# Two weight pieces of an output projection in other buffers, and one shared buffer for the first turned probabilities of each head

## The chip, the cores and the metric

The kernel runs on one core of one Trainium2 chip. The metric is the device time of one execution in microseconds (us).

## The reference

One layer of a streaming encoder, for 1024 tokens of width 1024 and 256 memory tokens, in float32:

```python
# 1. token mixing: u, q, k, v, f = rms_norm(x) @ w_in, then
y_s = s5_mixer(u)                          # 32 groups x 16 channels, gated
y_f = forgetting_attention(q, k, v, f)     # 8 heads x 64, blocks of 128 queries, causal
y = concatenate([rms_norm(y_s), rms_norm(y_f)]) @ w_out
x = x + rms_norm(y, post_g)
# 2. cross-attention, 4 heads of 256, over 256 memory tokens
x = x + rms_norm(memory_cross_attention(rms_norm(x), mem_n, wq, wkv, wo))
# 3. x = x + rms_norm(swiglu(rms_norm(x), w_gate, w_up, w_down))
```

## The kernel before

**Products.** Every float32 product is made from a hi and a lo part: `split` writes hi on ScalarE (L113) and lo, the source less hi, on VectorE (L115; L117 where a gain is multiplied in), and three matmuls (L122 to L124) sum hi·hi, hi·lo and lo·hi. A 128 x 1024 weight piece is loaded by SyncE into a staging buffer (512 KB), split into a buffer of 8 KB per partition that holds both parts, and then multiplied.

**Buffers.** The pool `slab` has 16 buffers of 8 KB, `raw` (staging) 2, `whl` (split pieces) 3. The pool `t4` has buffers of 4 KB by tag: a 2, b 2, c 3, d 1, e 1, and smaller ones, t2 3 and yt 2. A new tile of a tag takes the oldest buffer, and whatever writes it first (mostly a load) waits until the old tile's last reader is done. PSUM has four banks `g` and, once attention is over, four banks `x`.

**Order.** The kernel is written once, and a scheduler with a timeline of its own decides in what order the instructions stand on each engine. Within an engine, and in SyncE's row of loads, the order is then fixed: what waits holds up everything behind it.

**Attention** (`fox`) runs 8 heads of 8 query tiles. `scores` makes probabilities in a tile `c`; `turn` transposes them on TensorE (L771) and splits the result into hi and lo for a pair of query tiles; `values` multiplies them with v (L782, L783). The squares of the result (ScalarE, L802) are summed by GpSimd (L803) into `d`, summed over channels by TensorE (L237), and give `r_f`, the scale of this branch for each token. Beside attention other work is stepped through as filler, among it cross-attention's `build_a`, which multiplies the query weights (`in_wqT`, loaded by `load_w`, L158) with the memory's keys.

**Output projection** (`wo` and the loop below it). The state-space half was done before and lies in HBM as `t1_d` (`t_d` in the profile). For the attention half, `w_out_f` comes in 4 pieces, staged in `raw` and split into `slab` (L1029). Then for each of 8 token tiles j: `xt` in a buffer c is loaded from x (L1038), `t` from `t1_d` (L1041); 2 x 12 products go into two banks `x`; VectorE adds them, scaled by `r_f`, onto `t` (L1048); ScalarE squares (L1050), GpSimd multiplies by a gain row (L1052); the squares are summed (L1054), and VectorE's last step (L1056) adds `t`, scaled, to `xt`, which GpSimd's queue stores (L1057). So `t` of tile j holds its buffer from its load to L1056. Its tag is "aab"[j % 3]: tiles 0, 1, 3, 4, 6, 7 take the two buffers a, tiles 2 and 5 take b.

**Behind it** stands cross-attention's value side: `wo` of cross-attention comes in pieces through `raw` and `e` (`raw<-in_wo`, `e<-in_wo`), is split into `whl`, and is multiplied into banks `g` and `x` (`g<-whl,b`, `x<-whl,b` at L122 to L124).

Of the kernel before, what the change touches and what calls it, by code (L numbers as in the profile page):

```python
# [17 lines left out]
P = 128  # L18
S = 1024
D = 1024  # L20
# [32 lines left out]
def layer(ctx: ExitStack, tc: tile.TileContext, a, out):  # L53
# [15 lines left out]
    def slab(shape, dt=F32R):  # L69
        return slabp.tile(shape, dt, name="slab", tag="slab")  # L70
# [4 lines left out]
    def raw(shape):  # L75
        return rawp.tile(shape, F32, name="raw", tag="raw")

    def g_ps(shape):
        return psg.tile(shape, F32, name="g", tag="g")
# [4 lines left out]
    def sm(n, name):  # L84
        return small.tile([P, n], F32, name=name, tag=name)
# [26 lines left out]
    def split(hi, lo, src, mul=None, lo_eng=None):  # L112
        first = act.activation(out=hi, in_=src, func=AF.Copy, scale=1.0 if mul is None else mul)  # L113
        if mul is None:
            (lo_eng or dve).tensor_tensor(out=lo, in0=src, in1=hi.bitcast(F32), op=ALU.subtract)  # L115
        else:
            dve.scalar_tensor_tensor(out=lo, in0=src, scalar=mul, in1=hi.bitcast(F32),  # L117
                                     op0=ALU.mult, op1=ALU.subtract)
        return first

    def mm3(ps, lh, ll, rh, rl, first, last):
        pe.matmul(ps, lh, rh, start=first, stop=False)  # L122
        pe.matmul(ps, lh, rl, start=False, stop=False)  # L123
        pe.matmul(ps, ll, rh, start=False, stop=last)  # L124

    def rsqrt_mean(r, ss, n, eps=EPS, ahead=None):

        w = r.shape[1]
        y, t, v = sm(w, "rsy"), sm(w, "rst"), sm(w, "rsv")
        if ahead is None:  # L130
            bias, half = epsc[:, 0:1] if eps == EPS else epsc[:, 1:2], -0.5 * eps
        else:
            e = sm(2, "rse")
            bias, half = e[:, 0:1], e[:, 1:2]
            dve.tensor_scalar(out=bias, in0=ahead, scalar1=1.0 / n, scalar2=eps, op0=ALU.mult, op1=ALU.add)
            dve.tensor_scalar(out=half, in0=bias, scalar1=-0.5, scalar2=None, op0=ALU.mult)
        act.activation(out=y, in_=ss, func=AF.Ln, scale=1.0 / n, bias=bias)
        last = act.activation(out=y, in_=y, func=AF.Exp, scale=-0.5)
        dve.tensor_scalar(out=v, in0=ss, scalar1=-0.5 / n, scalar2=half, op0=ALU.mult, op1=ALU.add)
        if w == 1:  # L140
            dve.scalar_tensor_tensor(out=t, in0=y, scalar=v, in1=y, op0=ALU.mult, op1=ALU.mult)
        else:
            dve.tensor_tensor(out=t, in0=y, in1=y, op=ALU.mult)
            dve.tensor_tensor(out=t, in0=t, in1=v, op=ALU.mult)
        done = dve.scalar_tensor_tensor(out=r, in0=t, scalar=1.5, in1=y, op0=ALU.add, op1=ALU.mult)
        return last, done
# [48 lines left out]
    def tt(tag, shape=None, dt=F32):  # L195
        return t4.tile(shape or [P, S], dt, name=tag, tag=tag, bufs=BUFS[tag])
# [508 lines left out]
    def fox(yf):  # L705
        heads, units, pts = {}, {}, {}
# [54 lines left out]
        def turn(h, t):  # L761
            tt = t % 2
            if tt == 0:
                pts[h, t // 2] = slab([P, 8, 256]), slab([P, 8, 256])
            pth, ptl = pts[h, t // 2]
            sc = units.pop((h, t))
            for k0 in range(0, t + 1, 4):
                n = min(4, t + 1 - k0)
                tp = g_ps([P, 4, P])
                for k in range(n):  # L770
                    pe.transpose(tp[:, k], sc[:, (k0 + k) * P:(k0 + k + 1) * P], ident)  # L771
                split(pth[:, k0:k0 + n, tt * P:(tt + 1) * P], ptl[:, k0:k0 + n, tt * P:(tt + 1) * P], tp[:, :n])
# [45 lines left out]
        for n in range(-lag, len(seq) + 1):  # L818
            if n + lag < len(seq):
                h, t = seq[n + lag]  # L820
                scores(h, t)
                if t == 1 and h + 1 < NH:
                    nxt = prepare(h + 1)
                if t % 2 and h + 1 < NH:
                    step(nxt)
                if t == 5 and h % 2 and h + 1 < NH:
                    load_v(h // 2 + 1)
            if 0 <= n < len(seq):
                h, t = seq[n]
                turn(h, t)  # L830
            yield
            if 0 < n:
                h, t = seq[n - 1]
                if t % 2:
                    values(h, t // 2)
                    if len(later) > 1 or h >= HA and later:
                        token_sums(*later.pop(0))
# [30 lines left out]
    def step(g, n=1):  # L868
        for _ in range(n):
            if next(g, "end") == "end":  # L870
                return
# [151 lines left out]
    def x_ps(shape):  # L1023
        return psx.tile(shape, F32, name="x", tag="x")

    wo = []
    for i in range(4):
        w = raw([P, D])
        sp.dma_start(out=w, in_=a["w_out_f"][i])  # L1029
        hl = slab([P, 2, D])  # L1030
        split(hl[:, 0], hl[:, 1], w)
        wo.append(hl)
    g_mp = gain_row(0, "d")
    a1 = build_a(1)
    for j in range(NT):
        ts = slice(j * P, (j + 1) * P)
        xt = tt("c")
        sp.dma_start(out=xt, in_=a["x"][ts, :])  # L1038
        t = tt("aab"[j % 3])
        for i in range(2):  # L1040
            sp.dma_start(out=t[64 * i:64 * i + 64], in_=t1_d.rearrange("j (k s) d -> s k j d", s=16)[2 * j + i])  # L1041
        ss4, ss, r = sm(4, "ss4"), sm(1, "ss"), sm(1, "r")
        for h in range(2):
            hs = slice(h * 512, h * 512 + 512)
            ps = x_ps([P, 512])
            for k in range(4):
                mm3(ps, yf[k][:, 0, ts], yf[k][:, 1, ts], wo[k][:, 0, hs], wo[k][:, 1, hs], k == 0, k == 3)
            dve.scalar_tensor_tensor(out=t[:, hs], in0=ps, scalar=r_f[:, j:j + 1], in1=t[:, hs], op0=ALU.mult, op1=ALU.add)  # L1048
            for q in range(2 * h, 2 * h + 2):
                act.activation(out=tt("yt", [P, 256]), in_=t[:, q * 256:q * 256 + 256], func=AF.Square,  # L1050
                               accum_out=ss4[:, q:q + 1])
            pool.tensor_tensor(out=t[:, hs], in0=t[:, hs], in1=g_mp[:, hs], op=ALU.mult)  # L1052
            step(a1)
        dve.tensor_reduce(out=ss, in_=ss4, op=ALU.add, axis=mybir.AxisListType.X)  # L1054
        rsqrt_mean(r, ss, D)
        dve.scalar_tensor_tensor(out=xt, in0=t, scalar=r, in1=xt, op0=ALU.mult, op1=ALU.add)  # L1056
        stC.dma_start(out=x1_d[j], in_=xt)  # L1057
# [13 lines left out]
    xT, xr, pts, x1_read = {}, {}, {}, []  # L1071
# [235 lines left out]
    def ev():  # L1307
        return evp.tile([P, 512], F32, name="ev", tag="ev")
# [111 lines left out]
    for n in range(2):  # L1420
        w = ev()
# [185 lines left out]
```

## Time and profile before

| | before |
|---|---|
| median of 3 runs (lowest to highest) | 1432.37 us (1430.96 to 1433.04) |
| the profiled execution's own time | 1430.57 us |
| its span | 1428.8 us |
| mean granted TensorE clock | 0.992 |
| TensorE busy | 1390.7 us, 97% |
| VectorE, ScalarE, GpSimd busy | 70%, 50%, 29% |

The profile shows one execution; its times are counted from the start of its span. In a row, a name before `<-` is written and names behind it are read, with the numbers of buffers left out. A bracket behind a row is the time that the engine stood idle before it and the instruction that released it. The granted clock of TensorE is 1.00 at full speed.

### The profile page before, as it was taken

To read this page: it belongs to the slowest core of one execution; us is meant where nothing else is said; L and a number is where in the kernel's file an instruction comes from. 1 tells how busy PE (TensorE), PEld (TensorE's weight loads), DVE (VectorE), ACT (ScalarE), POOL (GpSimd) and SP (SyncE) were. 2 spreads that over 40 slices of the span, in tenths; PEclk is the share of its full clock that TensorE was granted. 3 is DMA by queue.
4 is the path that set the end of the run, shared out by engine and by line. 5 is a ranking of instruction groups with operands and counts; after the bars stand their busy time and mean duration, and the time that the engine had idled before them with its cause. 6 is when DMAs were issued, how large, how long until landed. Compare 5 with 4: busy or idle time off the path is not lost.

```text
span 1428.8 us, 20846 instructions
## 1 busy us (share of the span) xinstructions
PE 1390.7 (97%) x7422; PEld 1187.5 (83%) x7422; DVE 1003.7 (70%) x1818; ACT 708.0 (50%) x1421; POOL 410.9 (29%) x432
## 2 busy tenths in 40 slices
PE   7999999999999898999999999999999999999997
PEld 6889898889989886788888788888888888888886
DVE  7839947877888876645557677887766676565565
ACT  6373347777888754543434533333333334444341
POOL 0001000022243134001111367676666661000021
PEclk9999999999999999999999999999999999999999
DMA  6325654165654658323637455454444446965444
GB/s 204 98 80 148 183 192 132 33 204 178 193 153 120 172 164 276 134 74 109 193 112 236 149 190 173 168 181 154 164 156 162 162 155 227 334 219 192 177 162 162
DMA packets 112824, 238.43 MB, mean 167 GB/s; under 512 B 11848, under 2 KB 48712, under 8 KB 112592
## 3 DMA queue, kind: packets, MB, share of 16 engines
q1 hardware_dynamic: 96576, 182.01, 39.8%
q0 software_dynamic: 16144, 55.09, 10.6%
q8 instruction: 58, 0.95, 0.3%
q14 instruction: 46, 0.38, 0.1%
HBM read 168.90 MB, written 76.81 MB: 172 GB/s over the span
## 4 chain that ended last, share of the span: by engine, by line
PE 58%; DVE 1%; DMA 1%; ACT 0%; issue 0%; DVEq 0%; SPq 0%; ACTq 0%
PE x L1277 17%; PE g L1277 13%; PE x L1535 7%; PE g L1535 7%; PE x L123 2%; PE x L124 2%; PE x L122 2%; PE g L122 2%; PE g L124 2%; PE g L123 2%; PE g L1065 1%; DMA a<-t_d 1%; PE g L1173 1%; DVE slab L115 0%; DVE whl L115 0%; DVE c L1056 0%
## 5 line engine op out<-in xcount | busy, mean ns | idle before, releaser
L1277 PE MATMUL x<-slab,op 128*128 128x512 f32 x984 | 233.3, 389 | 0.5 <-DVE op L115 0.5
L1277 PEld LDWEIGHTS x<-slab,op 128*128 128x128 f32 x984 | 184.6, 188 | 39.3 <-DVE op L115 1.0
L1277 PE MATMUL g<-slab,op 128*128 128x512 f32 x744 | 178.7, 389 | 0.0
L115 DVE TENSOR_TENSOR slab<-slab 128x1024 fp32r<-128x1024 f32 (+2 forms) x92 | 110.2, 1207 | 84.7 <-ACT slab L113 82.8
L1277 PEld LDWEIGHTS g<-slab,op 128*128 128x128 f32 x744 | 139.6, 188 | 29.0
L122 PE MATMUL g<-slab,whl 128*128 128x512 f32 (+1 forms) x416 | 151.7, 365 | 0.6 <-ACT whl L113 0.4
L123 PE MATMUL g<-slab,whl 128*128 128x512 f32 (+1 forms) x416 | 148.4, 357 | 0.0
L124 PE MATMUL g<-slab,whl 128*128 128x512 f32 (+1 forms) x416 | 148.2, 357 | 0.0
L113 ACT ACTIVATE slab<-slab 128x1024 fp32r<-128x1024 f32 (+2 forms) x92 | 94.8, 1037 | 106.4 <-DMA slab<-hs_d 81.5
L1535 PE MATMUL g<-slab 128*128 128x512 f32 x462 | 126.6, 389 | 0.0
L1535 PE MATMUL x<-slab 128*128 128x512 f32 x462 | 126.6, 389 | 0.0
L1535 PEld LDWEIGHTS g<-slab 128*128 128x128 f32 x462 | 86.7, 188 | 18.0
L1535 PEld LDWEIGHTS x<-slab 128*128 128x128 f32 x462 | 86.7, 188 | 18.0
L122 PE MATMUL g<-whl,slab 128*128 128x256 f32 (+2 forms) x288 | 87.5, 309 | 9.6 <-ACT whl L113 7.3
L115 DVE TENSOR_TENSOR op<-slab,op 128x512 fp32r<-128x512 f32 x80 | 83.9, 1059 | 11.6 <-ACT op L113 11.3
L1353 POOL TENSOR_TENSOR wt<-wt 128x256 f32<-128x256 f32 x88 | 84.2, 957 | 19.9 <-DMA wt<-in_w_down 16.3
L113 ACT ACTIVATE op<-slab 128x512 fp32r<-128x512 f32 x80 | 50.0, 627 | 77.7 <-PE x L1277 37.5
L122 PEld LDWEIGHTS g<-slab,whl 128*128 128x128 f32 x416 | 78.6, 189 | 11.8 <-ACT whl L113 0.6
L124 PEld LDWEIGHTS g<-slab,whl 128*128 128x128 f32 x416 | 78.4, 189 | 11.6 <-DVE whl L115 0.2
L115 DVE TENSOR_TENSOR whl<-raw,whl 128x1024 fp32r<-128x1024 f32 (+2 forms) x61 | 72.0, 1184 | 22.3 <-ACT whl L113 21.7
L123 PEld LDWEIGHTS g<-slab,whl 128*128 128x128 f32 x416 | 78.6, 189 | 10.6
L123 PE MATMUL g<-whl,slab 128*128 128x256 f32 (+2 forms) x288 | 86.1, 299 | 0.0
(394 smaller groups left out, 3149.3 us busy)
## 6 DMA issues: line engine op xcount, KB each, us to landing
hs_d<-ev POOLq DMA_DIRECT2D x77, 256.0 KB, 2.6
slab<-hs_d SPq DMA_DIRECT2D x35, 512.0 KB
wt<-in_w_down SPq DMA_DIRECT2D x44, 256.0 KB
wt_d<-wt POOLq DMA_DIRECT2D x22, 512.0 KB, 4.8
slab<-in_w_gate SPq DMA_DIRECT2D x20, 512.0 KB
slab<-in_w_up SPq DMA_DIRECT2D x20, 512.0 KB
slab<-wt_d SPq DMA_DIRECT2D x20, 512.0 KB
wd_d<-in_w_down SPq DMA_DIRECT2D x33, 256.0 KB
```

What stands on the lines that cost most here:

```text
L113: first = act.activation(out=hi, in_=src, func=AF.Copy, scale=1.0 if mul is None else mul)
L115: (lo_eng or dve).tensor_tensor(out=lo, in0=src, in1=hi.bitcast(F32), op=ALU.subtract)
L122: pe.matmul(ps, lh, rh, start=first, stop=False)
L123: pe.matmul(ps, lh, rl, start=False, stop=False)
L124: pe.matmul(ps, ll, rh, start=False, stop=last)
L1065: pe.transpose(tp[:, k], src[:, (k0 + k) * P:(k0 + k + 1) * P], ident)
L1173: turned = pe.transpose(tp[:, k], h3[:, (4 * n + k) * P:(4 * n + k + 1) * P], ident)
L1277: pe.matmul(ps, x[:, k], y[:, k], start=first and k + n == 0, stop=k == 3 and n == 2, skip_group_check=not first)
L1353: pool.tensor_tensor(out=o, in0=x, in1=y, op=ALU.subtract)
L1535: pe.matmul(banks[n][j], xo[:, u, js], wo[:, v], start=ends[0] and k == 0, stop=ends[1] and k == 2, skip_group_check=onto is not None)
```

## The change

The first two query tile pairs of each head (t < 4) put hi and lo of the turned probabilities into one slab, each with room for four key tiles, so a head takes six slabs for them and not eight. Pieces 2 and 3 of `w_out_f` are staged in a buffer a and a buffer c of `t4`, not in `raw`. The tag of `t` is "baa"[j % 3]: tiles 0, 3 and 6 take b, tiles 1, 2, 4, 5 and 7 take a. So tile 3 no longer follows another tile of the loop in its buffer; tile 4 follows tile 1, tile 5 tile 2, tile 6 tile 0, and tile 7 tile 4, as before. Lines behind the first edit move down by four (L1041 is L1045 in the change, L1056 is L1060).

```diff
@@ -761,7 +761,11 @@
         def turn(h, t):
             tt = t % 2
             if tt == 0:
-                pts[h, t // 2] = slab([P, 8, 256]), slab([P, 8, 256])
+                if t < 4:
+                    both = slab([P, 2, 4, 256])
+                    pts[h, t // 2] = both[:, 0], both[:, 1]
+                else:
+                    pts[h, t // 2] = slab([P, 8, 256]), slab([P, 8, 256])
             pth, ptl = pts[h, t // 2]
             sc = units.pop((h, t))
             for k0 in range(0, t + 1, 4):
@@ -1025,7 +1029,7 @@
 
     wo = []
     for i in range(4):
-        w = raw([P, D])
+        w = raw([P, D]) if i < 2 else tt("ac"[i - 2])
         sp.dma_start(out=w, in_=a["w_out_f"][i])
         hl = slab([P, 2, D])
         split(hl[:, 0], hl[:, 1], w)
@@ -1036,7 +1040,7 @@
         ts = slice(j * P, (j + 1) * P)
         xt = tt("c")
         sp.dma_start(out=xt, in_=a["x"][ts, :])
-        t = tt("aab"[j % 3])
+        t = tt("baa"[j % 3])
         for i in range(2):
             sp.dma_start(out=t[64 * i:64 * i + 64], in_=t1_d.rearrange("j (k s) d -> s k j d", s=16)[2 * j + i])
         ss4, ss, r = sm(4, "ss4"), sm(1, "ss"), sm(1, "r")
```

SyncE's row of loads around 475 to 500 us, before (`a` and `b` from `t1_d` are `t` of the projection's tiles, a_5936 tile 0, a_6046 tile 1, b_6391 tile 5; raw_5917, raw_5922 and raw_5927 are pieces 1, 2 and 3 of `w_out_f`; raw_5970 is the first piece of `in_wqT`):

```order
L1041 DMA a_5936<-t1_d_112 64x1x1024
L1029 DMA raw_5917<-in_w_out_f 128x1024
L1041 DMA a_5936<-t1_d_112 64x1x1024
L1208 DMA t2_6622<-kv_d_113 128x2x256
L1041 DMA b_6391<-t1_d_112 64x1x1024 x2
L1038 DMA c_5934<-in_x 128x1024
L1038 DMA c_6044<-in_x 128x1024
L1041 DMA a_6046<-t1_d_112 64x1x1024 x2
L1029 DMA raw_5922<-in_w_out_f 128x1024
L1029 DMA raw_5927<-in_w_out_f 128x1024
L1038 DMA c_6135<-in_x 128x1024
L158 DMA raw_5970<-in_wqT 128x1024
```

and in the change (a_5906 and c_5911 are pieces 2 and 3, b_6227 is tile 3, a_6030 tile 1, a_6121 tile 2, raw_5954 and raw_5959 are the first two pieces of `in_wqT`):

```order
L1033 DMA a_5906<-in_w_out_f 128x1024
L1033 DMA raw_5901<-in_w_out_f 128x1024
L1212 DMA t2_6606<-kv_d_113 128x2x256
L1045 DMA b_6227<-t1_d_112 64x1x1024 x2
L1033 DMA c_5911<-in_w_out_f 128x1024
L1042 DMA c_5918<-in_x 128x1024
L1045 DMA a_6030<-t1_d_112 64x1x1024 x2
L158 DMA raw_5954<-in_wqT 128x1024
L158 DMA raw_5959<-in_wqT 128x1024
L1045 DMA a_6121<-t1_d_112 64x1x1024 x2
L1042 DMA c_6028<-in_x 128x1024
L1042 DMA c_6119<-in_x 128x1024
```

Piece 2 has taken the place of tile 0's load (which went further ahead, into a buffer b), piece 3 stands ahead of the first load of x, tile 3's load stands where tile 5's did, and the two places in `raw` that pieces 2 and 3 held go to `in_wqT`.

ScalarE's row at the end of attention, before (slab_5799 is the hi part of the last head's last turned probabilities, from g_5851 the first half and from g_5858 the second; slab_5924 and slab_5929 are pieces 2 and 3 of `w_out_f`; whl_5971 is the first piece of `in_wqT`; L802 makes the squares that GpSimd sums):

```order
L113 ACTIVATE slab_5919<-raw_5917 128x1024
L113 ACTIVATE slab_5477<-g_5814,gains_98 128x256
L789 ACTIVATE yt_5844<-g_5831 64x256
L113 ACTIVATE slab_5799<-g_5851 128x4x128
L113 ACTIVATE slab_5477<-g_5814,gains_98 128x256
L113 ACTIVATE slab_5250<-yt_5844,gains_98 64x256
L802 ACTIVATE yt_5844<-yt_5844 64x256
L113 ACTIVATE slab_5924<-raw_5922 128x1024
L113 ACTIVATE slab_5799<-g_5858 128x4x128
L113 ACTIVATE slab_5929<-raw_5927 128x1024
L113 ACTIVATE whl_5971<-raw_5970 128x1024
L789 ACTIVATE yt_5882<-g_5865 64x256
```

and in the change (slab_5783, from g_5835 and g_5842, is the same hi part; slab_5908 and slab_5913 are pieces 2 and 3; whl_5955 and whl_5960 are the first two pieces of `in_wqT`; the squares are L806):

```order
L113 ACTIVATE slab_5903<-raw_5901 128x1024
L113 ACTIVATE slab_5908<-a_5906 128x1024
L113 ACTIVATE slab_5463<-g_5798,gains_98 128x256
L113 ACTIVATE slab_5913<-c_5911 128x1024
L793 ACTIVATE yt_5828<-g_5815 64x256
L113 ACTIVATE slab_5783<-g_5835 128x4x128
L113 ACTIVATE whl_5955<-raw_5954 128x1024
L113 ACTIVATE slab_5463<-g_5798,gains_98 128x256
L113 ACTIVATE slab_5783<-g_5842 128x4x128
L113 ACTIVATE whl_5960<-raw_5959 128x1024
L113 ACTIVATE slab_5236<-yt_5828,gains_98 64x256
L806 ACTIVATE yt_5828<-yt_5828 64x256
```

Pieces 2 and 3 stand ahead of the first half of the last evacuation; ahead of its second half stands the first piece of `in_wqT`, where piece 2 stood, and ahead of the squares of yt_5828 its second piece.

SyncE's row of loads in the projection's loop, before (a_6243, a_6334, a_6448 and a_6505 are `t` of tiles 3, 4, 6 and 7; the c tiles are x for tiles 3 to 7 in order; e_6627 and e_6683 are pieces of cross-attention's `wo`):

```order
L1041 DMA a_6243<-t1_d_112 64x1x1024 x2
L1041 DMA a_6334<-t1_d_112 64x1x1024 x2
L1038 DMA c_6241<-in_x 128x1024
L1208 DMA t2_6739<-kv_d_113 128x2x256
L158 DMA e_6627<-in_wo 128x1024
L1038 DMA c_6332<-in_x 128x1024
L158 DMA raw_6678<-in_wo 128x1024
L1038 DMA c_6389<-in_x 128x1024
L1041 DMA a_6448<-t1_d_112 64x1x1024 x2
L158 DMA e_6683<-in_wo 128x1024
L1038 DMA c_6446<-in_x 128x1024
L1041 DMA a_6505<-t1_d_112 64x1x1024 x2
```

and in the change (b_6432 is tile 6, a_6318 tile 4, a_6375 tile 5, a_6489 tile 7; e_6611 and e_6667 are the pieces of `wo`):

```order
L1045 DMA b_6432<-t1_d_112 64x1x1024 x2
L1045 DMA a_6318<-t1_d_112 64x1x1024 x2
L1042 DMA c_6225<-in_x 128x1024
L1045 DMA a_6375<-t1_d_112 64x1x1024 x2
L158 DMA e_6611<-in_wo 128x1024
L1042 DMA c_6316<-in_x 128x1024
L158 DMA raw_6662<-in_wo 128x1024
L1042 DMA c_6373<-in_x 128x1024
L1212 DMA t2_6723<-kv_d_113 128x2x256
L158 DMA e_6667<-in_wo 128x1024
L1045 DMA a_6489<-t1_d_112 64x1x1024 x2
L1042 DMA c_6430<-in_x 128x1024
```

Tile 3's load is gone from here, tiles 6, 4 and 5 stand ahead of the first e piece, and tile 7's load still stands behind the second.

## Rows read from the trace of the kernel before

**Rows 1.** The page of the profile: the line of the busy times (busy us, share of the span, instructions), TensorE's busy tenths in 40 slices of 35.7 us, and the chain of work that ended last, by engine.

```profile
PE 1390.7 (97%) x7422; PEld 1187.5 (83%) x7422; DVE 1003.7 (70%) x1818; ACT 708.0 (50%) x1421; POOL 410.9 (29%) x432
...
PE   7999999999999898999999999999999999999997
...
PE 58%; DVE 1%; DMA 1%; ACT 0%; issue 0%; DVEq 0%; SPq 0%; ACTq 0%
```

**Rows 2.** The busy time by stretch: start and end in us, length, then for each engine the busy us and its instructions, the granted clock of TensorE (1.00 is full), the share of the DMA engines in use and GB/s.

```profile
505.00:510.00 5.00, 5.00 (x17) 3.96 (x16) 1.64 (x2) 2.48 (x3) 0.00 (x0) 0.70 0.51 161
...
540.00:545.00 5.00, 4.65 (x20) 3.86 (x21) 4.12 (x8) 4.16 (x14) 2.77 (x2) 1.00 1.00 285
545.00:550.00 5.00, 4.13 (x17) 2.74 (x15) 4.52 (x8) 2.05 (x6) 1.45 (x2) 1.00 0.89 328
...
570.00:575.00 5.00, 3.39 (x7) 2.28 (x8) 4.52 (x7) 4.97 (x10) 1.51 (x2) 0.50 0.84 249
575.00:580.00 5.00, 5.00 (x21) 4.04 (x21) 5.00 (x7) 4.58 (x10) 0.00 (x0) 0.87 0.95 374
```

**Rows 3.** The timeline of SyncE's queue, on which the loads are issued: start, length, line, what is loaded from where; a row with x2 or x4 holds so many issues, from the first one's start to the last one's end.

```profile
417.37 0.45 SPq L722 DMA_DIRECT2D e<-qk_d  x1
...
420.82 0.41 SPq L807 DMA_DIRECT2D slab<-v_d  x1
...
475.72 0.58 SPq L1041 DMA_DIRECT2D a<-t_d  x1
...
487.08 2.80 SPq L1038 DMA_DIRECT2D c<-in_x  x2
...
492.42 1.86 SPq L1029 DMA_DIRECT2D raw<-in_w_out_f  x2
...
502.97 8.67 SPq L158 DMA_DIRECT2D raw<-in_wqT  x4
...
530.90 3.37 SPq L1041 DMA_DIRECT2D a<-t_d  x4
...
538.11 0.42 SPq L158 DMA_DIRECT2D e<-in_wo  x1
...
556.71 1.23 SPq L1041 DMA_DIRECT2D a<-t_d  x2
```

**Rows 4.** The timeline of ScalarE: start, length, line, what is written from what; in brackets the idle time before the row and what ended it.

```profile
422.30 0.63 ACT L726 ACTIVATE a<-e 128x512 fp32r<-128x512 f32 x1 [1.27 <-DMA e<-qk_d]
...
500.63 1.06 ACT L113 ACTIVATE slab<-raw 128x1024 fp32r<-128x1024 f32 x1 [4.83 <-DMA raw<-in_w_out_f]
501.59 0.58 ACT L113 ACTIVATE slab<-g 128x512 fp32r<-128x512 f32 x1
...
548.56 1.06 ACT L113 ACTIVATE whl<-e 128x1024 fp32r<-128x1024 f32 x1 [1.51 <-DMA e<-in_wo]
...
570.23 1.04 ACT L113 ACTIVATE whl<-raw 128x1024 fp32r<-128x1024 f32 x1
```

**Rows 5.** The timeline of TensorE, two of the products of the output projection at the full clock, the first row behind the wait at 502 us, and the rows from 540 to 575 us that stand behind an idle time of over 0.2 us.

```profile
498.12 0.39 PE L123 MATMUL x<-slab 128*128 128x512 f32 x1
498.34 0.39 PE L124 MATMUL x<-slab 128*128 128x512 f32 x1
...
502.22 0.38 PE L782 MATMUL g<-slab 128*128 128x256 f32 x1 [1.97 <-ACT slab L113]
...
540.35 0.50 PE L122 MATMUL x<-slab 128*128 128x512 f32 x1 [0.48 <-DVE a L1048]
...
550.26 0.50 PE L122 MATMUL x<-slab 128*128 128x512 f32 x1 [1.07 <-DVE a L1048]
...
566.26 0.50 PE L122 MATMUL x<-whl,b 128*128 128x512 f32 x1 [0.75 <-DVE a L1048]
...
568.62 0.50 PE L122 MATMUL x<-whl,b 128*128 128x512 f32 x1 [1.39 <-DVE a L1048]
...
571.32 2.08 PE L122 MATMUL x<-whl,b 128*128 128x512 f32 x4 [1.72 <-ACT whl L113]
573.69 0.80 PE L123 MATMUL x<-whl,b 128*128 128x512 f32 x1 [0.29 <-DVE whl L115]
```

**Rows 6.** The timeline of VectorE: the first rows of tiles 0, 3, 4 and 7 of the output projection, the last steps of tiles 0 and 4, and the lo parts of three weight pieces (501.72 output projection, 550.13 and 572.42 cross-attention).

```profile
501.72 1.23 DVE L115 TENSOR_TENSOR slab<-raw,slab 128x1024 fp32r<-128x1024 f32 x1 [4.83 <-ACT slab L113]
...
516.29 0.16 DVE L145 SCALAR_TENSOR_TENSOR r_f<-rst,rsy 128x8 f32<-128x8 f32 x1
...
528.67 2.21 DVE L1056 SCALAR_TENSOR_TENSOR c<-a,r,c 128x1024 f32<-128x1024 f32 x1
...
539.55 0.75 DVE L1048 SCALAR_TENSOR_TENSOR a<-x,r_f,a 128x512 f32<-128x512 f32 x1 [3.80 <-DMA a<-t_d]
...
545.35 0.75 DVE L1048 SCALAR_TENSOR_TENSOR a<-x,r_f,a 128x512 f32<-128x512 f32 x1 [1.14 <-DMA a<-t_d]
...
550.13 1.21 DVE L115 TENSOR_TENSOR whl<-e,whl 128x1024 fp32r<-128x1024 f32 x1
...
555.40 1.28 DVE L1056 SCALAR_TENSOR_TENSOR c<-a,r,c 128x1024 f32<-128x1024 f32 x1
...
565.46 0.75 DVE L1048 SCALAR_TENSOR_TENSOR a<-x,r_f,a 128x512 f32<-128x512 f32 x1 [3.11 <-DMA a<-t_d]
...
572.42 1.22 DVE L115 TENSOR_TENSOR whl<-raw,whl 128x1024 fp32r<-128x1024 f32 x1
```

## The prediction

> **What bounds the kernel now.** The page comes first: TensorE is busy for 97% of the span and the chain that ended last is TensorE for almost all of what it could be followed through [rows 1]. No other engine is near its limit, so the change can only move TensorE's idle time and the stretches in which its clock is low. I therefore looked for both in the stretch that the edits touch, from 490 to 590 us; in the page's 40 slices TensorE is at 9 tenths or more from the seventeenth on to the last but one [rows 1], so what is won before that should go to the end undiminished.
>
> The table by stretch shows three disturbed places [rows 2]: a granted clock of 0.70 between 505 and 510, missing busy time between 540 and 550, and between 570 and 575 only 3.39 us busy at a clock of 0.50 (all of it the lower level, 1.2 of 2.4 GHz; 0.70 and 0.87 are mixes), then 0.87. The timeline of TensorE names the waits [rows 5]. First, 1.97 us at 502.22 for ScalarE's evacuation of the last attention probabilities. Second, 0.48 and 1.07 us at 540.35 and 550.26 for VectorE's first operation on tiles of the output projection. Third, 0.75, 1.39, 1.72 and 0.29 us from 566 to 574, first for the same operation on tile 7, then for a weight piece of cross-attention.
>
> Each has a late load behind it. ScalarE works through its row in order: it stood 4.83 us for `raw<-in_w_out_f` and then, at 501.59, did the evacuation that TensorE waited for [rows 4]; that load was issued at 492.42 [rows 3], so it took 8.2 us. VectorE's first operation on tiles 3, 4 and 7 waited 3.80, 1.14 and 3.11 us for `a<-t_d` [rows 6]. These loads went out only at 530.90 and 556.71 [rows 3], behind the last step of an older tile in the same buffer: tile 0's (528.67 plus 2.21) and tile 4's (555.40 plus 1.28) [rows 6].
>
> **The shared buffer in attention.** No instruction is added or removed, and the rows of TensorE and ScalarE stay nearly as they were until 490 us. I cost it at nothing, because no wait listed above is one for a free 8 KB buffer. It has one side effect: SyncE's last `slab<-v_d` now stands ahead of four `e<-qk_d` loads. Before, it went out at 420.82 and they from 417.37 [rows 3], so those loads come at most 3.5 us later. ScalarE already stood 1.27 us for one of them [rows 4]. The bounds are 0 (the buffer is free in time) and a loss of 3.5 us (all of it reaches TensorE); I take 0, because fewer buffers taken can only free one earlier.
>
> **Weight pieces 2 and 3 (term A).** They no longer queue for the two raw buffers. Piece 2 goes out where tile 0's `a<-t_d` stood (475.72), piece 3 where the first `c<-in_x` stood (487.08) [rows 3]. With the same 8.2 us, piece 3 lands at 495.3, and the 15 products of 512 columns that used to follow the wait come before it, at 0.22 to 0.23 us each [rows 5], or 3.4 us. But the places at 492.42 now hold cross-attention's first two pieces, and ScalarE's rows put the first ahead of the second half of the last evacuation and the second ahead of the squares that GpSimd sums. If the first lands when piece 2 did, at 500.6, ScalarE evacuates the half after its 1.0 us and a 0.5 us row, about 502.1 to 502.7. VectorE's lo part follows its own 1.2 us on the piece [rows 6], one short row and 0.7 us, about 504.0. TensorE, which was ready at 500.25 (502.22 less 1.97), is ready some 3.1 us later at 503.3, and idles about 0.7 us. The sum of squares behind the second piece costs an estimated 0.4 us more. So 1.97 becomes 1.1, a gain of 0.9. The low clock after the wait cost 5.00 times 0.30, or 1.5 us [rows 2]; with half the idle time I take 1.0 of it. A is -1.9, with bounds of 0 (the new wait is as long as the old) and -3.5 (all idle time and all the low clock go).
>
> **The turn "baa" (term B).** Tile 3 now takes the second b buffer and is loaded where tile 5 was, long before it is used, so its wait goes. Tile 4 and tile 5 follow tiles 1 and 2, tile 6 follows tile 0. But all three go out close together, around 528 to 533 us, where before there were two. Tile 4's load, second in the queue, will land around 541, as tile 4's did at 545.35 [rows 6] less the earlier issue, and TensorE can run two tiles (5.4 us each at 24 products) on the four PSUM banks before it needs tile 4's. Of 0.48 and 1.07 I take -1.3, with bounds of -0.5 and -1.6.
>
> **Tile 7 (term C).** Its load still waits for tile 4's last step; all depends on how early that is. Before, VectorE split the piece `whl<-e` at 550.13 and only then came to that step at 555.40, since tile 5's operations lay between [rows 6]; ScalarE's part of the piece waited for `e<-in_wo` until 548.56 [rows 4], 10.4 us after its issue [rows 3]. In the change the piece still stands ahead. SyncE issues it behind loads that wait for tile 0's result, which comes about 3 us earlier, so the piece is split by about 548 and tile 4's step ends at 549.7 instead of 556.7. Tile 7's load took 8.75 us (556.71 to 565.46 [rows 3, 6]), so it lands at 558.5.
>
> From that landing to the hi part of the next weight piece ScalarE took 5.8 us (565.46 to 570.23 plus 1.04 [rows 4, 6]), and to the lo part 8.2 us (572.42 plus 1.22 [rows 6]): 564.3 and 566.7. TensorE without its own waits would need the hi part at 567.5 (571.32 less 1.72, 1.39 and 0.75 [rows 5]); less A and B that is 564.3, and the lo part four products later, 565.2. So the hi part is just in time and the lo part 1.5 us late: 4.15 us of idle time become 1.5. The clock cost 3.39 times 0.50 and 5.00 times 0.13 [rows 2], 2.35 us; I take 1.35 of it as won. C is -4.0. Its bounds are -1.0 (the landing comes 3 us later) and -6.5 (it comes by 557).
>
> **Sum.** -1.9 - 1.3 - 4.0 = -7.2 us. The profiled execution took 1430.57 us and would take 1423.4; the median of the three runs, 1432.37, lies 1.8 above it, so on the median's footing 1425.2 us.
>
> **A rule against the row.** The 8.2 us of the weight piece is the price on which A and C turn. The Trainium skill, "DMA: Bandwidth & Descriptors", section "Anatomy of one DMA — SWDGE (gpsimd) path", fits a transfer as about 2.0 us plus its bytes over 436 GB/s, which for 512 KB is an estimated 3.2 us (for loads that GpSimd issues; these are SyncE's). The rows show 8.2, 8.75 and 10.4 us with other loads in flight, and they decide. By the rule the first piece would be there before it is wanted, A would be -3.5 and C -6.5, and the sum -11.4 or so.
>
> **Rivals.** (1) Full gain: as the early loads no longer meet the crowd at 530.90, the pieces and tile 7 land within 6 us. Then the waits at 502 and from 566 on go whole: -3.5 - 1.5 - 6.5 = -11.5, 1420.9 us. For it: the DMA engines are in use for only half of 505 to 510; against: they are full from 540 to 545 [rows 2]. The Trainium skill's fit, above, would mean this case. (2) Tile 7 late: the e piece lands no earlier than before although it is issued earlier, because three loads of 512 KB run ahead of it at a DMA share of 1.00 [rows 2]. Tile 4's step then stays near 552, and C is only -1.0: -4.2, 1428.2 us. (3) Waits that change places: cross-attention's first piece lands 2 us later than piece 2 did, A falls to 0, C to 0, and only B is left: 1431.1 us. (4) Slower: that piece in front of ScalarE's last evacuation. TensorE has nothing else in its row there, so each us by which the piece lands later than 500.6 costs one us. The forecast turns into a loss of over 2.9 us when it lands later than 510.7 (1435.3 less 1425.2 is 10.1), 18.3 us after its issue; at 22 us it gives 1439. Against it: the slowest load in the rows, tile 4's, took 11 to 14 us. That the buffers change nothing at all is part of (3): then waits stand where they stood.
>
> **Chances.** The forecast 0.45 (its own range 1422.5 to 1427); (1) 0.10; (2) 0.24; (3) 0.15; (4) 0.06. A measurement of this kernel tells 0.2%, 2.9 us, from no change. Faster: the forecast, (1) and nearly all of (2), 0.78; same: (3) and the edge of (2), 0.16; slower 0.06. The range reaches from the full gain at 1420.5 to 1430.5, where half of (3) and all of (4) are left out.
>
> **What would show it.** A: ScalarE's row after 495 us without the 4.83 us wait for `raw<-in_w_out_f`, a shorter one for `raw<-in_wqT`, and a clock above 0.70 right after. B: no wait of VectorE for tile 3's load, no idle time of TensorE around 540. C: tile 4's last step before 551, tile 7's first operation before 560 us, and a clock above 0.50 in the 5 us that follow. Wrong it would be with an idle time of TensorE of over 2 us between 502 and 510, with tile 7's load landing after 562, or with new idle time in attention near 425 us.

## The result

| | before | the change |
|---|---|---|
| median of 20 runs each on one chip (lowest to highest) | 1431.21 us (1427.21 to 1434.09, but for one run) | 1434.63 us (1431.42 to 1439.45) |
| ratio to before, 95% interval | 1 | 1.0028 [1.002, 1.0035] |
| the profiled execution | 1430.57 us | 1434.69 us |
| its span, mean granted clock | 1428.8 us, 0.992 | 1432.9 us, 0.992 |

The change makes the kernel slower by 4.0 us (0.0028 of 1431.2); 1425.2 was predicted, and the range ended at 1430.5. One of before's runs took 2814.81 us; the ratio leaves it out. Gains and losses of kernels below are ratios to before on the same chip, times 1431.2 us, and what one kernel gains over another is the difference of two such ratios; the intervals of most are 1 to 2 us wide on either side.

**Where it went.** The page of the change, to be read against [rows 1], has TensorE just as busy:

```profile
PE 1392.8 (97%) x7422; PEld 1190.1 (83%) x7422; DVE 997.4 (70%) x1818; ACT 708.2 (49%) x1421; POOL 408.6 (29%) x432
```

Two places tell the story, first before, then in the change:

```profile
483.93 0.40 PE L782 MATMUL g<-slab 128*128 128x256 f32 x1 [1.80 <-DVE slab L115]
...
585.45 1.03 PE L1065 MATMUL g<-ident,c 128*128 128x128 f32 x8
```

```profile
482.94 0.36 PE L786 MATMUL g<-slab 128*128 128x256 f32 x1 [1.79 <-DVE slab L115]
...
589.03 1.03 PE L1069 MATMUL g<-ident,c 128*128 128x128 f32 x8
```

At the wait near 483 us the change is 1.0 us ahead. Behind the projection, at TensorE's first product with `ident,c`, it is 3.6 behind. The stretch between lost 4.6 us. TensorE's timeline in the change, the rows behind an idle time (in brackets), against [rows 5]:

```profile
503.94 0.39 PE L786 MATMUL g<-slab 128*128 128x256 f32 x1 [1.86 <-ACT slab L113]
...
505.34 0.58 PE L787 MATMUL g<-slab 128*128 128x256 f32 x1 [0.86 <-DVE slab L115]
...
521.39 0.50 PE L122 MATMUL x<-slab 128*128 128x512 f32 x1 [1.46 <-DVE b L1052]
...
553.04 0.50 PE L122 MATMUL x<-slab 128*128 128x512 f32 x1 [1.00 <-DVE a L1052]
...
561.43 0.50 PE L122 MATMUL x<-slab 128*128 128x512 f32 x1 [2.61 <-DVE a L1052]
...
571.98 0.50 PE L122 MATMUL x<-whl,b 128*128 128x512 f32 x1 [0.47 <-ACT b L113]
...
573.01 0.50 PE L124 MATMUL x<-whl,b 128*128 128x512 f32 x1 [0.29 <-DVE b L115]
...
577.09 0.50 PE L123 MATMUL x<-whl,b 128*128 128x512 f32 x1 [0.60 <-DVE whl L115]
...
585.82 1.19 PE L122 MATMUL x<-whl,b 128*128 128x512 f32 x4 [0.69 <-ACT whl L113]
```

And the table by stretch, against [rows 2] (the granted clock is the third number from the end):

```profile
505.00:510.00 5.00, 4.66 (x22) 4.66 (x23) 2.27 (x3) 1.09 (x3) 0.80 (x1) 0.50 0.81 270
510.00:515.00 5.00, 5.00 (x24) 4.86 (x24) 1.89 (x3) 2.20 (x4) 0.00 (x0) 0.55 0.15 27
...
560.00:565.00 5.00, 3.57 (x10) 2.86 (x11) 3.82 (x8) 1.99 (x10) 3.10 (x3) 0.73 0.78 228
...
570.00:575.00 5.00, 4.23 (x18) 2.88 (x17) 4.39 (x8) 3.86 (x13) 3.57 (x3) 1.00 0.57 173
```

Up to 522 us TensorE idles 1.86 + 0.86 + 1.46 = 4.18 us where it idled 1.97, and after the first two waits it runs ten microseconds at about half the clock: 4.66 x 0.50 + 5.00 x 0.45 = 4.6 us lost, against 1.5 before. From 540 on the idle time is 5.66 us where it was 5.70, and the clock costs about 1.0 us (3.57 x 0.27) and not 2.35. So the front of the stretch lost 5.3 us, and of the 5.3 us that B and C were to bring at its end only about 1.4 came; 0.7 of the 4.6 us stay without a place, 0.2 of them a clock of 0.93 from 565 to 570. This is one execution. The kernels e9, e14 and e18 below differ from the change only further on in the loop or behind it, and in their traces `r_f`, which comes at 520.38 in the change, comes at 520.26, 518.68 and 516.30; so what one trace shows of this front holds to a few us only.

The late work at the front is on ScalarE:

```profile
501.98 1.06 ACT L113 ACTIVATE whl<-raw 128x1024 fp32r<-128x1024 f32 x1 [7.26 <-DMA raw<-in_wqT]
...
503.30 0.59 ACT L113 ACTIVATE slab<-g 128x512 fp32r<-128x512 f32 x1
504.11 1.06 ACT L113 ACTIVATE whl<-raw 128x1024 fp32r<-128x1024 f32 x1 [0.23 <-DMA raw<-in_wqT]
...
505.72 0.42 ACT L806 ACTIVATE yt<-yt 64x256 f32<-64x256 f32 x1
511.41 1.06 ACT L113 ACTIVATE whl<-raw 128x1024 fp32r<-128x1024 f32 x1 [5.27 <-DMA raw<-in_wqT]
...
514.74 0.41 ACT L806 ACTIVATE yt<-yt 64x256 f32<-64x256 f32 x1
...
519.42 0.29 ACT L137 ACTIVATE rsy<-sv_f,epsc 128x8 f32<-128x8 f32 x1
```

The wait of 4.83 us for a piece of the projection [rows 4] has become one of 7.26 us for a piece of cross-attention, in front of the same evacuation (503.30). A third piece, with 5.27 us of waiting, stands in front of the last squares (514.74), from which `r_f` is made. `r_f` is then ready at 520.38 and not at 516.29 [rows 6], and the whole projection follows it. Further on, SyncE's loads and VectorE's rows:

```profile
534.54 1.23 SPq L1045 DMA_DIRECT2D b<-t_d  x2
536.58 1.56 SPq L1045 DMA_DIRECT2D a<-t_d  x2
...
542.69 0.40 SPq L158 DMA_DIRECT2D e<-in_wo  x1
...
560.74 1.23 SPq L1045 DMA_DIRECT2D a<-t_d  x2
```

```profile
520.38 0.17 DVE L145 SCALAR_TENSOR_TENSOR r_f<-rst,rsy 128x8 f32<-128x8 f32 x1
...
548.12 0.75 DVE L1052 SCALAR_TENSOR_TENSOR a<-x,r_f,a 128x512 f32<-128x512 f32 x1 [4.12 <-DMA a<-t_d]
...
556.72 1.22 DVE L115 TENSOR_TENSOR whl<-e,whl 128x1024 fp32r<-128x1024 f32 x1 [1.30 <-ACT whl L113]
...
559.43 1.28 DVE L1060 SCALAR_TENSOR_TENSOR c<-a,r,c 128x1024 f32<-128x1024 f32 x1
...
568.82 0.75 DVE L1052 SCALAR_TENSOR_TENSOR a<-x,r_f,a 128x512 f32<-128x512 f32 x1 [1.72 <-PE g L124]
```

The loads go out 3.6 us later than before (534.54 against 530.90 [rows 3]), the `e` piece is split at 556.72 where 548 was expected, tile 4's last step starts at 559.43 and not by 548.4, and tile 7's first operation at 568.82.

### The profile page after: what moved, and what is told of

Same layout as the page of the kernel before. It is cut to its first block, busy times and chain, and to the rows that moved or that the text cites. A ratio compares the mean times of both kernels' runs of the same rounds, so it can differ in the third digit from the quotient of the medians.

```text
span 1432.9 us, 20850 instructions
## 1 busy us (share of the span) xinstructions
PE 1392.8 (97%) x7422; PEld 1190.1 (83%) x7422; DVE 997.4 (70%) x1818; ACT 708.2 (49%) x1421; POOL 408.6 (29%) x432
## 4 chain that ended last, share of the span: by engine, by line
PE 80%; DVE 10%; DMA 4%; ACT 4%; issue 2%; SPq 0%; POOL 0%; DVEq 0%; ACTq 0%; POOLq 0%
PE x L1281 17%; PE g L1281 13%; PE x L1539 7%; PE g L1539 7%; PE g L122 6%; PE g L124 6%; PE g L123 6%; PE x L123 2%; PE x L124 2%; PE x L122 2%; PE g L775 2%; DMA raw<-in_wqT 1%; DVE whl L115 1%; DVE slab L117 1%; PE g L1069 1%
## 5 line engine op out<-in xcount | busy, mean ns | idle before, releaser
L122 PE MATMUL g<-whl,slab 128*128 128x256 f32 (+2 forms) x288 | 87.8, 310 | 11.5 <-ACT whl L113 7.9
```

## The experiments

The three parts are called W (weight pieces 2 and 3 staged in a and c), B (the turn "baa") and S (the shared slab). Each kernel below was timed in several rounds beside before.

| kernel | parts and additions | ratio to before | us |
|---|---|---|---|
| e1_wo_only | W | 1.0005 [0.9994, 1.0015] | +0.7 |
| e2_baa_only | B | 0.9997 [0.9987, 1.0006] | -0.4 |
| e3_slab_only | S | 0.9976 [0.9965, 0.9988] | -3.4 |
| e4_hold | S, W, B, hold | 0.9992 [0.9982, 1.0003] | -1.1 |
| e5_wo_and_baa | W, B | 1.0039 [1.0024, 1.0054] | +5.6 |
| e6_slab_and_wo | S, W | 0.9997 [0.9988, 1.0006] | -0.4 |
| e7_slab_and_baa | S, B | 0.9997 [0.9987, 1.0006] | -0.4 |
| e8_hold_aab | S, W, hold | 0.9956 [0.9942, 0.9969] | -6.3 |
| e9_late6 | S, W, B, tile 6's load later | 1.0022 [1.0013, 1.0032] | +3.1 |
| e10_hold_late6 | S, W, B, hold, tile 6's load later | 1.0003 [0.9993, 1.0013] | +0.4 |
| e11_hold_until_third | S, W, shorter hold | 0.9997 [0.9987, 1.0008] | -0.4 |
| e12_hold_no_slab | W, hold | 0.9972 [0.996, 0.9983] | -4.0 |
| e13_hold_e | S, W, B, hold, e piece's split later | 0.9985 [0.9977, 0.9994] | -2.1 |
| e14_after_e | S, W, B, e piece's split later | 1.0032 [1.0019, 1.0044] | +4.6 |
| e15_hold_aab_e | S, W, hold, e piece's split later | 0.9971 [0.9959, 0.9983] | -4.2 |
| e16_hold_vh | e4_hold, `vh` of head 1 moved | 0.9977 [0.9968, 0.9986] | -3.3 |
| e17_hold_e_vh | e13_hold_e, `vh` of head 1 moved | 0.9972 [0.996, 0.9983] | -4.0 |
| e18_after_e_vh | e14_after_e, `vh` of head 1 moved | 1.0018 [1.0007, 1.0029] | +2.6 |

Two theories stood at the start. T1: cross-attention's pieces, let into `raw` early, stand in ScalarE's row ahead of the last evacuation and the last squares, and make `r_f` late. T2: the turn "baa" sends three loads of `t` at once, and the crowd makes the `e` piece, and with it tile 7, late.

**Each part alone.** One hunk of the diff each; in short:

```diff
# W
-        w = raw([P, D])
+        w = raw([P, D]) if i < 2 else tt("ac"[i - 2])
# B
-        t = tt("aab"[j % 3])
+        t = tt("baa"[j % 3])
# S
+                    both = slab([P, 2, 4, 256])
+                    pts[h, t // 2] = both[:, 0], both[:, 1]
```

> Only the staging of weight pieces 2 and 3 (one of the three edits), the rest as before. Theory 1 (ScalarE's order): the two raw buffers that become free let cross-attention's first pieces in, and ScalarE takes them ahead of the last evacuation and of the squares; so this edit alone is slower than before by 3 to 5 us, with a wait of about 7 us of ScalarE for raw<-in_wqT near 500 us and r_f near 520 instead of 516. Theory 2 (a crowd of loads): three loads of t at once delay the later pieces; they need the other turn of the tags, so this edit alone is within 2 us of before. Theory 3 (the shared buffer) gives no change here either.

> Only the turn "baa" of the tags of t. Theory 1: no loss; the wait for tile 3's load goes (0.5 to 1.6 us), so 0 to 3 us faster than before. Theory 2: tiles 4, 5 and 6 are loaded together, the e piece and tile 7 come later, 2 to 4 us slower than before. Theory 3: no change.

> Only the shared buffer for the turned probabilities. Theories 1 and 2: within 1.5 us of before, rather faster (the 0.85 us wait near 426 us was gone in the changed kernel's trace). Theory 3 (another order in attention costs the time): 3 us slower than before.

W and B each leave the time as it was, so neither theory's loss shows in a part alone; S gains 3.4 us, more than was expected. Added, the parts would bring -3.1 us; together they cost 4.0. W alone does have what T1 describes: ScalarE stands 4.87 and 6.18 us for `raw<-in_wqT`, `r_f` comes at 518.59, and TensorE idles 4.64 us between 500 and 520, against 1.97 before. But it no longer idles at 540 and 550 (1.55 us before), and 1.3 us less ahead of 490. In S the last `slab<-v_d` load goes out at 413.71 and not at 420.82 [rows 3], TensorE's wait of 0.85 us at 426 for an evacuation of ScalarE is gone, and the wait at 500 is smaller and costs no clock, where before the clock fell to 0.70 behind it and 1.5 us were lost [rows 2]. Why S gains is not shown: e1 and e5, without S, idle only 0.2 us near 426 too.

```profile
413.71 0.40 SPq L811 DMA_DIRECT2D slab<-v_d  x1
```

```profile
499.68 0.39 PE L786 MATMUL g<-slab 128*128 128x256 f32 x1 [1.04 <-ACT slab L113]
```

```profile
505.00:510.00 5.00, 4.54 (x28) 3.78 (x27) 3.70 (x4) 2.54 (x5) 0.79 (x1) 1.00 0.44 142
```

**Parts in pairs.** The same hunks, two at a time.

> The staging edit and the turn "baa" together, without the shared buffer. If the edits add up, 0.3 to 0.7 us above before (each alone was within 1 us): 1431 to 1433. If the late scale r_f of the staging edit and the crowd of three loads of the turn make each other worse (theory 4), 3 to 6 us slower than before: 1434 to 1437.

> Shared buffer and staging edit, with the old turn "aab". If the edits add up, 2 to 4 us faster than before: 1427 to 1429. Theory 4 (staging and turn together cost) says the same. If the shared buffer and the staging edit work against each other (theory 5: what the shared buffer wins is a shorter wait at the end of attention, which the staging edit replaces), the gain is gone: 1431 to 1434.

> Shared buffer and the turn "baa", pieces 2 and 3 in raw. If the edits add up, or by theories 4 and 5, 2 to 4 us faster than before: 1427 to 1429. If it is above 1431, the turn takes back what the shared buffer wins (theory 6).

W and B together cost 5.6 us. S, which gains 3.4 alone, is worth 1.1 beside W and nothing beside B. The price of B read off pairs is -0.4 us alone, +3.0 behind S, +4.9 behind W and +4.4 behind S and W. The traces do not put it in one place. Behind W it lies behind `r_f`: this comes at 518.59 in e1 and 517.18 in e5, the first `ident,c` at 585.21 and 587.57. In e7 TensorE loses ahead of it: it stands 4.48 us at 503.38, as ScalarE waits 7.41 us for `raw<-in_w_out_f`, where e3 had 1.04 and 3.88.

**The hold (T1).** ScalarE's part of the second `build_a`'s pieces stands behind the last square of attention, with nothing else changed:

```diff
-                act.activation(out=sq, in_=y, func=AF.Square)
+                sqs.append(act.activation(out=sq, in_=y, func=AF.Square))
...
-            wq = [load_w(a["wqT"][2 * hd + d], P) for d in range(2)]
+            with tc.issue_after(sqs[-1].ins) if c else ExitStack():
+                wq = [load_w(a["wqT"][2 * hd + d], P) for d in range(2)]
```

e8 has the turn "aab" beside it, e12 also goes without S, and e11 is e8 with `sqs[-2]`, the last square but one.

> The whole change, with ScalarE's parts of cross-attention's pieces (build_a(1)) held behind the last square of attention; loads stay free. Theory 1: the wait near 502 us goes, r_f comes before 512 us, and the time is 4 to 9 us below before (1422 to 1427). Theory 2: the crowd of loads stays, so it stays slower than before or at most 1 us faster, and the e piece still lands about 13 us after its issue.

> As the run with ScalarE's parts of cross-attention's pieces held behind the last square, but with the old turn "aab": two loads of t together, not three. If the crowd of loads takes back what the early r_f wins (theory 2 and 4), tile 4's load and the e piece land within 10 us of their issue and the time is 3 to 7 us below that run: 1423 to 1427. If the crowd does not matter, it is within 1.5 us of it, 1428.5 to 1431.5, with tile 3 waiting for its load again.

> As the best run so far (held pieces, turn "aab", 1424.2), but ScalarE's parts of the pieces stand behind the last square but one: the evacuations and the third square come first, the last one (and so r_f) stays behind the third piece. It tells apart what the early evacuation wins from what the early r_f wins. If the evacuation and the third sum are what counts, 1424 to 1426; if r_f is, 1428 to 1431, near the 1430.15 of the run with shared buffer and staging edit alone, with r_f after 515 us and idle time of TensorE around 511 to 519.

> As the best run so far, but without the shared buffer: staging edit, turn "aab", held pieces. If the shared buffer's gain (3.3 us alone) is one in attention, it is lost here: 1426.5 to 1429. If it was only a shorter wait for the pieces at the end of attention, which the held pieces replace, the time stays at 1423.5 to 1425.5.

The hold brings 5.2 us on the whole change (1.0028 to 0.9992) and 5.9 on S and W (0.9997 to 0.9956): that the pieces in this row cost so much is shown, and e8, at 1424.18 us, is faster than both kernels. e4 alone stays short of the 1422 to 1427 us that T1 had called for; with "baa" something more is lost. In e4 ScalarE does the last squares first, then the pieces, without waiting, and `r_f` is there 11.5 us earlier than in the change:

```profile
504.52 0.42 ACT L806 ACTIVATE yt<-yt 64x256 f32<-64x256 f32 x1
504.96 2.01 ACT L113 ACTIVATE whl<-raw 128x1024 fp32r<-128x1024 f32 x2
```

```profile
508.88 0.17 DVE L145 SCALAR_TENSOR_TENSOR r_f<-rst,rsy 128x8 f32<-128x8 f32 x1
```

Its TensorE has no idle time between 487 and 540. e11 splits T1: the evacuation of the probabilities is as early as in e8 (495.20 and 495.42), but the last value tile stands behind the third piece, and all 5.9 us are lost again. Not only its square is late (`r_f` at 516.58, in e8 at 508.32): so is the evacuation of its bank `g` (L793, L794). ScalarE in e11, then in e8:

```profile
507.62 1.06 ACT L113 ACTIVATE whl<-raw 128x1024 fp32r<-128x1024 f32 x1 [5.56 <-DMA raw<-in_wqT]
508.70 0.38 ACT L793 ACTIVATE yt<-g 64x256 f32<-64x256 f32 x1
```

```profile
502.58 0.38 ACT L793 ACTIVATE yt<-g 64x256 f32<-64x256 f32 x1 [5.59 <-PE g L787]
```

So it is the third piece ahead of the last value tile, not the evacuation of the probabilities, that costs. TensorE in e11 waits first for that bank, then for `r_f`; the two were not tried apart:

```profile
510.43 0.58 PE L122 MATMUL g<-e,whl 128*128 128x256 f32 x1 [2.73 <-DVE yt L794]
...
517.59 0.50 PE L122 MATMUL x<-slab 128*128 128x512 f32 x1 [1.41 <-DVE a L1054]
```

e12 against e8 puts S at 2.3 us there, just inside the intervals.

**The crowd of loads (T2).** Tile 6's load goes behind tile 4's load of x in SyncE's row, on the whole change and on e4:

```diff
+            with tc.issue_after(xin[4].ins) if j == 6 else ExitStack():
+                sp.dma_start(out=t[64 * i:64 * i + 64], in_=t1_d.rearrange("j (k s) d -> s k j d", s=16)[2 * j + i])
```

> The whole change, with one thing moved: SyncE issues tile 6's load of t only behind tile 4's load of x, so that two loads of t and not three stand ahead of the e piece. Theory 2 and 4 (the crowd): tile 4's load lands within 9.5 us of its issue, the e piece within 10 us instead of 12.9, and the time falls by 2 to 4 us, to 1430.5 to 1432.5. If the loss of the pair of edits comes from the late r_f alone, it stays within 1.2 us of the changed kernel (1433.4 to 1435.8).

> The held pieces (early r_f), the turn "baa", and tile 6's load behind tile 4's load of x. If both causes are the right ones, this is near the best run: 1422 to 1426, as tile 3 need not wait for its load and the crowd is smaller. If moving one load does not help, it stays at the 1430 of the first run with held pieces.

Neither is faster than the kernel it was made from (-0.9 and +1.6 us, both within the intervals), although tile 4's load comes earlier. In e4 (first fence) and e10 (second), TensorE's wait for tile 4 falls from 2.76 to 0.49 us, and two later ones grow by about 2 us each:

```profile
543.02 0.79 PE L122 MATMUL x<-slab 128*128 128x512 f32 x1 [2.76 <-DVE a L1054]
...
553.32 0.50 PE L122 MATMUL x<-slab 128*128 128x512 f32 x1 [0.24 <-DVE a L1054]
...
568.43 0.79 PE L122 MATMUL x<-whl,b 128*128 128x512 f32 x1 [6.66 <-ACT b L113]
```

```profile
541.25 0.50 PE L122 MATMUL x<-slab 128*128 128x512 f32 x1 [0.49 <-DVE a L1055]
...
552.66 0.50 PE L122 MATMUL x<-slab 128*128 128x512 f32 x1 [2.52 <-DVE a L1055]
...
571.41 0.79 PE L122 MATMUL x<-whl,b 128*128 128x512 f32 x1 [8.65 <-ACT b L113]
```

So moving this one load does not win back the price of "baa". The crowd itself is not excluded by it: the `e` piece still took 11.8 us in e9 and 13.9 in e10, where T2 had called for less than 10.

**The rows behind the e piece.** In the change the piece's split stands in ScalarE's and VectorE's rows ahead of tile 4's last step and tile 5's second half. Here it stands behind them:

```diff
+                if 2 * h + d == 2:
+                    for i in (adds[11], ends[4], squares[23]):
+                        behind.enter_context(tc.issue_after(i.ins))
```

> The kernel of e4_hold (1430.0) with one more order held: ScalarE's and VectorE's split of the first piece of cross-attention's wo staged in e stands behind tile 4's last step, tile 5's additions and tile 5's squares (in e4_hold it stood ahead of them). E (the turn baa costs because that piece's load goes out behind two t loads, lands 12 to 15 us after its issue, and tile 4's last step, tile 5's banks and tile 7's load stand behind it in the rows): the last step of tile 4 comes 2 us earlier or more than in e4_hold, tile 7's load with it, and the time falls to 1424 to 1427. C (what baa costs is the loads themselves, their landing and not the rows behind the e piece): within 1.2 us of e4_hold, 1429 to 1431.

> The whole change, with the split of the first e piece held as in e13_hold_e and nothing else held. E: 1431 to 1432.5 (from about 1434.6), as the waits of 1.0 and 2.6 us at 553 and 561 shrink. C: within 1.2 us of the change, 1433.5 to 1435.8.

> The kernel of e8_hold_aab (1424.2, the old turn aab) with the split of the first e piece held behind tile 4's last step and tile 5's second half as in e13_hold_e. E: under aab the piece landed 7 us after its issue and nothing waited for it, so nothing is won or at most 1.5 us: 1422.5 to 1424.5. C: the same within 1.2 us. If it comes out slower by over 1.5 us, holding the piece has a price of its own, which is then to be taken off what e13_hold_e shows.

The steps come out of the piece's way, but the time gains at most 1 us: -1.0 us on e4, +0.6 on the change, both inside the intervals, and +2.1 on e8, where these touch. In e14 tile 4's last step does come earlier (555.42, in the change 559.43). In e13 it does not (553.94, in e4 553.19), as its load itself lands at 543.96 and not at 542.22. The expectation that this is the cause fell as to time; but if the 2.1 us that the order costs on e8 are its price under "baa" too, as the expectation of e15 would have it, the rows are worth up to 3 us and not 1. The trace of e13 shows what stands behind it (ScalarE, then TensorE):

```profile
568.41 0.63 ACT L113 ACTIVATE b<-t 128x512 fp32r<-128x512 f32 x1 [0.28 <-DVE c L1062]
...
569.14 1.04 ACT L113 ACTIVATE whl<-raw 128x1024 fp32r<-128x1024 f32 x1
```

```profile
569.10 0.79 PE L122 MATMUL x<-whl,b 128*128 128x512 f32 x1 [6.25 <-ACT b L113]
```

`b<-t` is `vh`, the values of cross-attention's head 1, and its tag is b. Under "aab" the last tile of the loop in a buffer b is tile 5; under "baa" it is tile 6, the last but one. So `vh` waits for tile 6's last step (`DVE c L1062`), and the next weight piece stands behind it on ScalarE. In every kernel with "baa" and this buffer the row stands at 566 to 573 us; in those with "aab" at 555 to 562, as in e8:

```profile
555.47 0.64 ACT L113 ACTIVATE b<-t 128x512 fp32r<-128x512 f32 x1 [1.04 <-DVE c L1062]
```

**The buffer of vh.** Head 1's `vh` goes to a buffer a, behind tile 5 as under "aab":

```diff
-        vh = tt("b", [P, 2, 2, 256], F32R)
+        vh = tt("a" if h == 1 else "b", [P, 2, 2, 256], F32R)
```

> The kernel of e4_hold (1430.0) with one buffer moved: cross-attention's values of head 1 (vh) in a buffer a, behind tile 5, where they stood in a buffer b. V (the tag b has a user behind the loop: under aab vh of head 1 follows tile 5 in its buffer, under baa it follows tile 6, whose last step is the last but one of the loop; in e4_hold ScalarE's b<-t waited for it until 567.75 and TensorE stood 6.66 us): the wait of 6.66 us is gone or under 2.5 us, head 1's products start 4 us earlier or more, and the time falls to 1425 to 1427.5 (head 2's vh now follows tile 6 and may cost part of it). Rival D (the loads of the tiles land late whatever takes b, and bound the stretch): a wait of the same size shows up for tile 7's load or the next piece, and the time stays within 1.2 us of e4_hold.

> The kernel of e13_hold_e (1429.3, wait of 6.25 us for b<-t at 569) with vh of head 1 in a buffer a. V: 1424.5 to 1427; if the rows behind the e piece cost something too, it comes out below e16_hold_vh by 1 us or more. D: within 1.2 us of e13_hold_e.

> The kernel of e14_after_e (1435.2, wait of 6.34 us for b<-t at 573) with vh of head 1 in a buffer a. V: 1430 to 1432.5, as that wait falls below 3 us. D: within 1.2 us of e14_after_e.

It gains 2.1, 1.9 and 2.0 us over the kernel that each was made from; only the first of these lies outside its interval, and just so, but three alike are taken as real. V named a cause but was too high, as 2.5 to 5 us had been expected, and part of what rival D says came true. In e16 TensorE's waits for this head become one of 3.29 us for the next piece, which still stands behind head 2's `vh` and tile 6, and tile 4's load costs 4.18 us:

```profile
543.43 0.50 PE L122 MATMUL x<-slab 128*128 128x512 f32 x1 [4.18 <-DVE a L1054]
...
568.83 2.08 PE L122 MATMUL x<-whl,a 128*128 128x512 f32 x4 [3.29 <-ACT whl L113]
```

With both rows moved, "baa" (e17, 0.9972) takes what "aab" takes with the e piece held (e15, 0.9971). Of the 5.2 us that "baa" costs between e8 and e4, 2 are the buffer of `vh`; the e piece's rows are worth about 1 (e4 to e13, e16 to e17), inside the intervals and with the reserve above; the last 2 are not settled. The nearest candidate is tile 4's load behind tile 6's in the queue: e10 took that wait away, but there the wait for `vh` had taken its place. e10 with `vh` moved wasn't tried. Another one is `vh` of head 0, which takes a buffer b too and under "baa" follows tile 3, not tile 2: its row stands at 552.36 in the change, behind 2.54 us of waiting for tile 3's last step, and at 534.38 before. It was left where it was.

## Why the prediction was wrong, point by point

**Bound and place: right.** TensorE's idle time and its clock between 490 and 590 us decide, and the three places are the ones where the change moved it most.

**Shared buffer (0): wrong, by -3.4 us alone.** The bounds held no gain. The step that failed is "no wait listed above is one for a free 8 KB buffer": the list began at 490 us, and the 0.85 us at 426 and SyncE's `v_d` load 7 us earlier stood outside it. The waits in e3 explain the gain in part only: 1.0 us near 426 and 1.5 of clock from 505 to 510, and why these follow from the buffer stays open. In the change 1.0 us of it is left at 483, and W and B spend that.

**Term A (-1.9): the sign was wrong; measured +5.3** (2.2 idle, 3.1 clock). The wait for the projection's pieces did go, and the first new piece landed at 501.98, only 1.4 us after the 500.6 assumed. The step that failed is the 0.4 us for the sum of squares: ScalarE's row was read down to the squares of one value tile. One tile further a third piece stands ahead of the last tile's evacuation and squares; it cannot be loaded before the first pieces leave `raw`, goes out at 504.32 and is there at 511.41. `r_f` came 4.1 us later, where C had counted on tile 0's result some 3 us earlier, a figure that it takes from no row: 7 us on the one number on which C rests. e4 and e8 show that these pieces in the row cost over 5 us, e11 that the third alone does. The change's own trace cannot part the loss between the pieces: of its 5.3 us, 1.5 are the wait for `r_f`, and 0.8 of idle time and 3.1 of clock come with the two waits behind the first pieces. (The sum also puts 15 products at 3.4 us and then goes on with 3.1; that is 0.3 us of idle time.)

**Term B (-1.3): right as to tile 3, not as to the rest.** The idle time at 540 is gone. But that the loads of tiles 6, 4 and 5 go out together was not harmless: tile 4's landed at 548.12, VectorE waiting 4.12 us, not at 541.

**Term C (-4.0): wrong.** Its chain was rightly drawn, and rival (2) named the place, though it had the piece issued earlier: the `e` piece, issued 4.6 us later than before, took 12.9 us to 555.63 where 10.4 had been used, and tile 4's step started at 559.43. B and C together brought 1.4 us and not 5.3. What the chain lacked was the second user of tag b behind the loop: with "baa" cross-attention's `vh` waits for tile 6. In the change itself TensorE stands only 0.47 us for it, since the other waits come first; in e4, e13 and e14, where some of these were moved away, it came out at 6.3 to 6.7 us (4.3 in e9, 8.7 in e10).

**Rivals.** The slower case was given 0.06 and put on the first piece landing after 510.7; it landed at 501.98, and by e11 the third is enough for the loss. The Trainium skill, "DMA: Bandwidth & Descriptors", section "Anatomy of one DMA — SWDGE (gpsimd) path", would have a 512 KB load there in an estimated 3.2 us (about 2.0 us plus the bytes over 436 GB/s, for loads that GpSimd issues); SyncE's loads in this trace do not keep to it, with 10.0 us for the first piece and 12.9 for `e`, among other loads. With them the full gain, rival (1), fell.

## What to carry to other kernels

Freeing a staging buffer lets in whatever is next in the queue, and an engine that works in order then waits for that load in front of rows that others need: follow the row down to the last instruction of the result that everything else awaits (here the last value tile, and `r_f` behind it), not to the first that looks harmless. When a buffer's turn is changed, list every user of its tag, those behind the loop too, and see which tile each now follows. Time the parts alone and in pairs: here parts worth +0.7, -0.4 and -3.4 us cost 4.0 together, and two of them, S and W, with the row order mended gain 6.3.

## What was not expected of the hardware

The same load of 512 KB into `e`, issued by SyncE, took from 5.6 us (e6, 542.49 to 548.12) to 14.9 us (e4, 532.92 to 547.86). A full DMA share does not tell how much is moved: between 540 and 545 us the engines had a busy share of 1.05 in e10 and 0.98 in e8, and moved 255 and 386 GB/s.

```profile
540.00:545.00 5.00, 4.51 (x20) 3.40 (x19) 2.40 (x7) 2.12 (x9) 2.59 (x2) 1.00 1.05 255
```

```profile
540.00:545.00 5.00, 5.00 (x24) 4.14 (x23) 4.55 (x11) 3.52 (x13) 2.78 (x3) 1.00 0.98 386
```

After waits of 1.86 and 0.86 us that ended 1.4 us apart, TensorE was granted the lower level (0.50, 1.2 of 2.4 GHz) between 505 and 510 and 0.55 between 510 and 515 while it was busy for 4.66 and 5.00 us; this cost more than the two waits did.
